# The attention branch product as seven half-size products, its weights prepared earlier, the pooling branch gated on its way out of PSUM

## The chip, the cores and the metric

The kernel runs on one core of one Trainium2 chip. The metric is the time of one execution on the device in microseconds; the kernel before takes 1549.38 us, the median of 3 runs (1548.54 to 1550.18). PE is TensorE (PEld its weight loads), DVE is VectorE, ACT is ScalarE, POOL is GpSimd, and SP is SyncE, which here only issues DMAs.

## The reference, cut to what matters

One residual layer on x of 1024 tokens by 1024 channels, in float32. A pooling branch and a differential attention branch are each projected to 1024 channels, multiplied by their sigmoid gates, and added; then come an output projection and an MLP.

```
gates = jax.nn.sigmoid(h @ w_gate[l] + b_gate[l])
merged = (gates[..., :D_MODEL] * (y_pool @ w_branch_pool[l])
          + gates[..., D_MODEL:] * (y_attn @ w_branch_attn[l]))
x = x + merged @ w_out[l]

h2 = rmsnorm(x, g_ffn[l])
x = x + jnp.square(jax.nn.relu(h2 @ w_up[l])) @ w_down[l]
```

`y_attn` is 1024 tokens by 1024 (8 heads of 128), `w_branch_attn` is 1024 by 1024, `y_pool` is 1024 by 512.

## The kernel before

All products work on digits: `split` makes of a float32 tile a high part (a cast to fp32r on ACT) and a low part (a subtraction on DVE, or on POOL for most weights), and `mm3` adds three matmuls, high x high, high x low, low x high (L126 to L128), into one bank of PSUM. There are eight banks of 128x512.

The stages in order of time:

- **Heads** (until about 626 us). For each of 8 heads and 8 blocks of 128 tokens: the q/k/v projection (tile z), its preparation (a root mean square with POOL's `ms`, the scaling `qn` on DVE and POOL), transposes of q and k (tile tk), scores, exponentials, transposes of the scores, the product with v. The stages of several token blocks are in flight at once; the list `ORDER` sets their lags. Each head's output y goes to DRAM (`y_dram`), its row factors to `r_dram`.
- **Gate columns and pooling groups**, written behind the heads in the program and taken up by PE between their work, and alone until 701 us. A gate column is two fills of 24 matmuls; its bias is added on ACT (`go`, L757) and the result, not yet through the sigmoid, is stored in `g_dram`. The pooling branch's results go to `p_dram`.
- **Pooling products** (tile bp, 701 to 745 us): 8 blocks of 128 output channels by two halves of 512 tokens, 4 depth steps each. ACT copies each bank to `mp`. Meanwhile the heads' y are loaded, multiplied by their row factors (`y_scaled`) and split (`yT`), and the weights of the attention branch are loaded and split (`load_cols`).
- **Attention products** (tile ba, 745 to 832 us): again 8 blocks by two halves, with 8 depth steps. DVE multiplies the bank by its gate (`mg`, L844), POOL adds the gated pooling part (L845), and ACT and DVE split the sum into `mT`. The pooling part is gated in place on DVE (`mp`, L837).
- **Output projection** (tile op, from 832 us), first for tokens 0 to 511, then the rest; behind it the norm and the MLP, whose two large products already are made of seven half-size products each (`SIDES`, `u_product`, `d_product`).

The framework orders each engine's instructions by a planner: a ready instruction that was written earlier in the program goes first. On the chip each engine, and each DMA queue, then works strictly in the planned order. Nearly all loads are issued from SP's queue, so a load that waits for its buffer holds back the loads behind it.

Buffers that matter here: `W` (8 tiles, the head weights, later y and the branch weights), `fw` (4 tiles, the gate weights, later branch and output weights), `fr` and `fo` (2 tiles each, used in turn by `tmp`), `U` (11 tiles of the heads), `H` (`hp0` and `hp1`, first h, then the pooling operand, `mp` and `mT`).

Of the kernel before, what the change touches and what calls it, by code (L numbers as in the profile page):

```python
# [8 lines left out]
F32 = mybir.dt.float32  # L9
# [8 lines left out]
P = 128  # L18
# [19 lines left out]
N_QKVW = 8 * H  # L38
ROOMS = "WWFFWWWFFWWW"
N_AHEAD_Y = 4  # L40

# [16 lines left out]
def encoder_kernel(  # L58
# [31 lines left out]
    hp0 = [mix.enter_context(tc.tile_pool(name=f"hp0{i}", bufs=4)) for i in "ab"]  # L90
    hp1 = mix.enter_context(tc.tile_pool(name="hp1", bufs=8))
    wpool = mix.enter_context(tc.tile_pool(name="wpool", bufs=1))
# [7 lines left out]

    hcount = [0]

    def htile(shape, dt, name, th):

        if th == 0:
            hcount[0] += 1
        return (hp1 if th else hp0[(hcount[0] - 1) // 4 % 2]).tile(shape, dt, tag="H", name=name)

# [3 lines left out]
    def raw(shape, name):  # L112
        return rpool.tile(shape, F32, tag="raw", name=name)
# [4 lines left out]
    def split(hi, lo, src, lo_eng=None):  # L118

        nc.scalar.copy(hi, src)  # L120
        (lo_eng or nc.vector).tensor_tensor(lo, src, f(hi), op=ALU.subtract)  # L121
# [7 lines left out]

    wcount = [0]  # L130

    def wt(shape, name):

        wcount[0] += 1
        if wcount[0] > N_QKVW and ROOMS[(wcount[0] - N_QKVW - 1) // 2] == "F":
            return fw_tile(shape, name)
# [13 lines left out]

    def load_cols(src, c0, name, nk=NK):

        rw = raw([P, nk, P], f"r{name}")
        nc.sync.dma_start(rw, src[0 : nk * P, c0 : c0 + P].rearrange("(kk p) c -> p kk c", p=P))
        ws = []
        for j in range(0, nk, 4):
            w = wt([P, 2, 4, P], f"w{name}_{j}")
            split(w[:, 0], w[:, 1], rw[:, j : j + 4, :], nc.gpsimd)
            ws.append(w)
        return ws  # L160

    def load_cols2(src, c0, name):

        rw = raw([P, 4, 2 * P], f"r{name}")
        nc.sync.dma_start(rw, src[0 : 4 * P, c0 : c0 + 2 * P].rearrange("(kk p) c -> p kk c", p=P))
        ws = []
        for j in range(2):
            w = wt([P, 2, 4, P], f"w{name}_{j}")
# [48 lines left out]

    def gate(gts, c):
        for gt, c0, c1 in gts:
            nc.sync.dma_start(gt, g_dram[c * P : (c + 1) * P, c0:c1])  # L220
            nc.scalar.activation(gt, gt, AF.Sigmoid, bias=zero)

    def whole(g):
        return [(g, 0, S)], [g[:, 0:512], g[:, 512:S]]

    def pair(t):
        return t[:, 0, :], t[:, 1, :]

    def branch_pool(d, ws, ps_fn):

        m = htile([P, S], F32, f"mp{d}", 1)
        for th in range(2):
            ps = proj_T(ps_fn(f"bp{d}_{th}"), ws, lambda k, th: pair(ypT[k][th]), th, nk=4)
            nc.scalar.copy(m[:, th * 512 : (th + 1) * 512], ps)
        mp.append(m)
# [516 lines left out]
    def gate_cols(c):  # L752
        ws = fill_w(w_gate, c * P, f"gate{c}")
        for th in range(2):
            ps = fill_proj(ws, th, f"g{c}_{th}", spare_bank if c >= G_Z else fill_bank)
            fo = fo_tile(f"go{c}_{th}")
            nc.scalar.activation(fo[:, 0:512], ps, AF.Identity, bias=cols[:, c : c + 1])  # L757
            nc.scalar.dma_start(g_dram[c * P : (c + 1) * P, th * 512 : (th + 1) * 512], fo[:, 0:512])
            yield

    def gates():
        for c in range(2 * NK - 2):
            yield from gate_cols(c)
        for gen in [gate_cols(c) for c in (2 * NK - 2, 2 * NK - 1)] * 2:
            next(gen)
            yield

    gate_units = gates()
    for _ in range(G_FIRST):
        next(gate_units)  # L770
    for g in range(4):
        for _ in pool_group(g):
            next(gate_units)
    for _ in gate_units:
        pass


    vpool = attn.enter_context(tc.tile_pool(name="vpool", bufs=N_V))
    pb = mix.enter_context(tc.tile_pool(name="pb", bufs=5, space=PSUM))
    nbank = [0]  # L780

    def vt(shape, dt, name):
        return vpool.tile(shape, dt, tag="V", name=name)

# [9 lines left out]

    def yt_tile(d):
        fn = ut if d < N_YU else vt
        return lambda shape, dt, name, th: fn(shape, dt, name)
# [5 lines left out]
    nbank.append(0)  # L803


    def row_factors(d):
        if d < N_AHEAD_Y or d == 5:
            return [fu_tile(f"rb{d}")]
        if d == 4:
            return [ut([P, S], F32, f"rb{d}")]  # L810
        return [tmp(f"rb{d}_{i}") for i in range(2)]

    ws_bp = {0: load_cols2(w_branch_pool, 0, "bp0")}
    ys = {d: y_scaled(d, row_factors(d)) for d in range(N_AHEAD_Y)}
    ypT = [load_split(p_dram, g * P, f"ypT{g}", ypt_tile) for g in range(4)]
    mp, yT, ws_ba = [], [], {}

    for d in range(NK):
        if d % 2 == 0 and d + 2 < NK:
            ws_bp[d + 2] = load_cols2(w_branch_pool, (d + 2) * P, f"bp{d + 2}")  # L820
        elif d > NK - 4:
            j = len(ws_ba)
            ws_ba[j] = load_cols(w_branch_attn, j * P, f"ba{j}")
        branch_pool(d, ws_bp[d - d % 2][d % 2], bank)
        yT.append(split_halves(ys.pop(d), f"yT{d}", yt_tile(d)))
        if d + N_AHEAD_Y < NK:
            ys[d + N_AHEAD_Y] = y_scaled(d + N_AHEAD_Y, row_factors(d + N_AHEAD_Y))
    mT = {}
    for d in range(NK):
        if d + 3 < NK:  # L830
            ws_ba[d + 3] = load_cols(w_branch_attn, (d + 3) * P, f"ba{d + 3}")
        ws = ws_ba.pop(d)
        gp = [tmp(f"gp{d}_{th}") for th in range(2)]
        gate([(gp[0], 0, 512), (gp[1], 512, S)], d)
        for th in range(2):
            mh = mp[d][:, th * 512 : (th + 1) * 512]
            nc.vector.tensor_tensor(mh, mh, gp[th], op=ALU.mult)  # L837
        ga = fu_tile(f"ga{d}") if d % 2 else ut([P, S], F32, f"ga{d}")
        gate(whole(ga)[0], NK + d)
        for th in range(2):  # L840
            hs = slice(th * 512, (th + 1) * 512)
            ps = proj_T(bank(f"ba{d}_{th}"), ws, lambda k, th: pair(yT[k][th]), th)
            mg = tmp(f"mg{d}_{th}")
            nc.vector.tensor_tensor(mg, ps, ga[:, hs], op=ALU.mult)  # L844
            nc.gpsimd.tensor_tensor(mg, mg, mp[d][:, hs], op=ALU.add)  # L845
            t = htile([P, 2, 512], F32R, f"mT{d}_{th}", th)
            split(t[:, 0, :], t[:, 1, :], mg)
            mT[d, th] = t

    attn.close()
# [481 lines left out]
```

## Time and profile before

| | |
|---|---|
| median of 3 runs | 1549.38 us |
| the profiled execution | 1548.34 us, of which the span is 1546.6 us |
| PE busy / DVE / ACT / POOL | 1526.0 / 1012.4 / 816.5 / 350.9 us |
| pooling products | 701.5 to 745.2 us |
| attention products | 745.2 to 832.2 us |
| bytes moved | 206.41 MB, 133 GB/s over the span |

The profile comes from one execution. Its page gives each engine's busy time, the span in 40 slices, the chain of work that ended last, and groups of instructions by line, engine and tile. A row of a group reads: line, engine, operation, output<-inputs, shape, count | busy us, mean ns of one | idle time of the engine just before them, and who ended it. Other views give the busy time of each engine in chosen stretches, the instructions of one tile with their first and last start, the waits between engines, and the instructions of one engine in order of time. Matmuls overlap, and their ends are modelled, so the distance between starts tells more than a duration.

### The profile page before, as it was taken

The page shows a single profiled execution, that of the slowest core. Times are in us where ns is not written, and L with a number is a line of the kernel's source. Part 1 is how long each engine was busy: PE and PEld are TensorE (multiplying, and loading weights), DVE is VectorE, ACT ScalarE, POOL GpSimd, SP SyncE. Part 2 cuts the span into 40 slices and gives each one's busy share as a digit, 9 for nine tenths or more (in the row PEclk, how much of TensorE's full clock was granted, in tenths as well). Part 3 has the DMA queues.
Part 4 walks back from the last instruction along what each step waited for, and adds up shares of the span by engine and source line. Part 5 has one row for each costly group of instructions (what it writes and reads, how often), then busy time and mean ns, then how long its engine had stood idle before and what let it go on. Part 6 is the DMA issues. An engine that isn't in the chain of part 4 may idle for free.

```text
span 1546.6 us, 22053 instructions
## 1 busy us (share of the span) xinstructions
PE 1526.0 (99%) x7649; PEld 1320.4 (85%) x7649; DVE 1012.4 (65%) x2268; ACT 816.5 (53%) x1808; POOL 350.9 (23%) x448
## 2 busy tenths in 40 slices
PE   7999999999999999999999999999999999999999
PEld 6899999999998989888888887888888788888887
DVE  7777777777878787865322448766666668556672
ACT  6656555666666565566432546565555634333331
POOL 6433334243525262315443400000000000000000
PEclk9999999999999999999999999999999999999999
DMA  7111212020202031547426534555432789537650
GB/s 230 49 54 48 64 39 73 20 79 32 81 28 84 28 96 42 177 132 250 139 93 205 177 105 124 180 172 176 137 136 109 259 312 389 196 123 256 225 192 28
DMA packets 166681, 206.41 MB, mean 133 GB/s; under 512 B 10069, under 2 KB 102954, under 8 KB 166570
## 3 DMA queue, kind: packets, MB, share of 16 engines
q1 hardware_dynamic: 149162, 177.71, 34.8%
q10 hardware_dynamic: 17408, 27.30, 4.7%
q8 instruction: 60, 0.98, 0.3%
q14 instruction: 51, 0.42, 0.1%
HBM read 150.42 MB, written 54.56 MB: 133 GB/s over the span
## 4 chain that ended last, share of the span: by engine, by line
PE 91%; DVE 3%; issue 2%; ACT 1%; DMA 1%; POOL 1%; SPq 1%; POOLq 0%; DVEq 0%; ACTq 0%
PE z L126 5%; PE z L128 5%; PE z L127 5%; PE Da L126 4%; PE Da L127 4%; PE Da L128 4%; PE g L126 3%; PE g L127 3%; PE g L128 3%; PE Db L126 3%; PE Db L127 3%; PE Db L128 3%; PE X L126 2%; PE X L128 2%; PE X L127 2%; PE sc L512 2%
## 5 line engine op out<-in xcount | busy, mean ns | idle before, releaser
L126 PE MATMUL z<-wqkv,hT 128*128 128x384 f32 x512 | 174.5, 341 | 0.4 <-DVE qn L453 0.3
L128 PE MATMUL z<-wqkv,hT 128*128 128x384 f32 x512 | 174.1, 340 | 0.0
L127 PE MATMUL z<-wqkv,hT 128*128 128x384 f32 x512 | 173.8, 339 | 0.0
L522 ACT ACTIVATE s<-s,nm 128x256 f32<-128x256 f32 (+7 forms) x128 | 99.6, 778 | 45.8 <-DVE nm L514 42.7
L260 POOL TENSOR_TENSOR ms<-ms,mhalf 128x4 f32<-128x4 f32 x64 | 66.5, 1039 | 158.0 <-DVE ms L259 136.7
L126 PE MATMUL g<-hT,fwgate 128*128 128x512 f32 x256 | 101.0, 395 | 0.1
L127 PE MATMUL g<-hT,fwgate 128*128 128x512 f32 x256 | 101.0, 395 | 0.0
L128 PE MATMUL g<-hT,fwgate 128*128 128x512 f32 x256 | 101.0, 395 | 0.0
L126 PEld LDWEIGHTS z<-wqkv,hT 128*128 128x128 f32 x512 | 96.8, 189 | 3.9 <-DVE qn L453 1.0
L127 PEld LDWEIGHTS z<-wqkv,hT 128*128 128x128 f32 x512 | 96.6, 189 | 3.0
L128 PEld LDWEIGHTS z<-wqkv,hT 128*128 128x128 f32 x512 | 96.6, 189 | 2.2 <-DVE hT L121 0.5
L514 DVE CUSTOM_DVE_ANT_0 s<-sc,dist 128x512 f32<-128x512 f32 (+3 forms) x128 | 74.7, 586 | 19.7 <-PE sc L512 18.2
L121 POOL TENSOR_TENSOR wqkv<-rqkv,wqkv 128x384 fp32r<-128x384 f32 x60 | 64.0, 1085 | 19.2 <-ACT wqkv L120 15.5
L121 DVE TENSOR_TENSOR AS<-s,AS 128x512 fp32r<-128x512 f32 x64 | 43.9, 688 | 35.8 <-ACT AS L120 35.6
L511 PE MATMUL sc<-K,Q 128*128 128x512 f32 (+2 forms) x192 | 66.6, 353 | 0.1
L512 PE MATMUL sc<-K,Q 128*128 128x512 f32 (+2 forms) x192 | 66.5, 354 | 0.0
L459 POOL TENSOR_TENSOR qn<-qn,ggh 128x128 f32<-128x128 f32 x64 | 32.3, 505 | 138.7 <-DVE qn L453 127.7
L485 ACT CAST Q<-tk 64x128 fp32r<-64x128 f32 x128 | 33.2, 259 | 57.8 <-DVE Q L484 56.0
L482 ACT CAST Q<-tk 64x128 fp32r<-64x128 f32 x128 | 33.0, 258 | 53.7 <-DVE K L481 52.3
L121 POOL TENSOR_TENSOR fwgate<-frgate,fwgate 128x512 fp32r<-128x512 f32 x32 | 44.5, 1394 | 51.9 <-ACT fwgate L120 51.8
L128 PEld LDWEIGHTS g<-hT,fwgate 128*128 128x128 f32 x256 | 48.1, 188 | 8.6
L126 PEld LDWEIGHTS g<-hT,fwgate 128*128 128x128 f32 x256 | 48.2, 188 | 7.3 <-ACT go L757 0.4
(430 smaller groups left out, 4640.7 us busy)
## 6 DMA issues: line engine op xcount, KB each, us to landing
wd<-in_w_down_dram SPq DMA_DIRECT2D x56, 512.0 KB, 5.3
wu<-in_w_up_dram SPq DMA_DIRECT2D x32, 512.0 KB, 4.5
udS<-us SPq DMA_DIRECT2D x64, 256.0 KB, 2.4
ur<-udS SPq DMA_DIRECT2D x32, 512.0 KB, 3.3
rqkv<-in_w_in_dram SPq DMA_DIRECT2D x64, 192.0 KB, 2.7
ud<-u ACTq DMA_DIRECT2D x48, 256.0 KB, 2.1
ur<-ud SPq DMA_DIRECT2D x24, 512.0 KB, 4.7
frgate<-in_w_gate_dram SPq DMA_DIRECT2D x32, 256.0 KB, 2.6
```

Of the source, the lines that this page charges most:

```text
L121: (lo_eng or nc.vector).tensor_tensor(lo, src, f(hi), op=ALU.subtract)
L126: nc.tensor.matmul(ps, lhs_hi, rhs_hi, start=first, stop=False, **kw)
L127: nc.tensor.matmul(ps, lhs_hi, rhs_lo, start=False, stop=False, **kw)
L128: nc.tensor.matmul(ps, lhs_lo, rhs_hi, start=False, stop=last, **kw)
L260: nc.gpsimd.tensor_tensor(dst, dst, mhalf[:, :n], op=ALU.pow)
L459: nc.gpsimd.tensor_tensor(qn[:, 2:4, :], qn[:, 2:4, :], ggh.unsqueeze(1).broadcast_to([P, 2, HD]), op=ALU.mult)
L482: nc.scalar.copy(q_hi, q)
L485: nc.scalar.copy(Q[other, m, 1, :], q)
L511: nc.tensor.matmul(dst, Q[:, i, 0, :], rhs, start=True, stop=False)
L512: nc.tensor.matmul(dst, Q[:, i, 1, :], rhs, start=False, stop=True)
L514: nc.vector.tensor_tensor_reduce(out=s[i][:, c : c + w], in0=sc[:, 0:w], in1=dist[:, o0 + c : o0 + c + w], scale=2.0 ** -(h + 1), scalar=B ...
L522: nc.scalar.activation(s[i][:, 0:n], s[i][:, 0:n], AF.Exp, bias=last, scale=-1.0, accum_out=Z[:, i, t : t + 1])
```

## The change

The product of the 1024 by 1024 weights with the 1024 by 1024 y is taken apart into two by two halves and made of seven half-size products instead of eight, by sums of weight halves (side a) and of y halves (side b). A half-size product has 4 depth steps by 4 column blocks by 3 matmuls of 128x512. They run in the order 1, 2, 6, 7, 5, 4, 3 (`ORDER_BA`), in turn on two sets of four banks (`Xb`, `Yb`); 6, 5, 4 and 3 are added into what their banks hold.

- Side a: eight `weight_unit`s, hung on gate steps 3, 5, 6, 8, 9, 11, 12, 13, load pieces of `w_branch_attn`, make the sums on POOL and the digits on ACT and POOL, and store them in `wa_dram`. `load_a` loads one depth step's digits (512 KB) three steps ahead.
- Side b: all eight y are loaded and scaled and kept in `W`; `split_b` splits a half for one step, five steps ahead, and makes the sums in place on DVE.
- `after` takes each product out of PSUM: copies on ACT, additions, gating and splitting as before.
- The pooling branch is gated as it leaves PSUM (`gate_half`, DVE) instead of copied by ACT and gated later; gate halves come through `tmp`.

The diff, cut to its core:

```diff
-ROOMS = "WWFFWWWFFWWW"
-N_AHEAD_Y = 4
+N_AHEAD_B, N_AHEAD_A = 5, 3
+PREP_AT = (3, 5, 6, 8, 9, 11, 12, 13)
...
     def branch_pool(d, ws, ps_fn):
         m = htile([P, S], F32, f"mp{d}", 1)
+        gs_ = [gate_half(d, th) for th in range(2)]
         for th in range(2):
             ps = proj_T(ps_fn(f"bp{d}_{th}"), ws, lambda k, th: pair(ypT[k][th]), th, nk=4)
-            nc.scalar.copy(m[:, th * 512 : (th + 1) * 512], ps)
+            nc.vector.tensor_tensor(m[:, th * 512 : (th + 1) * 512], ps, gs_[th], op=ALU.mult)
         mp.append(m)
...
+    def weight_unit(src, digits, kk, ch):
+        cs = slice(ch * 256, (ch + 1) * 256)
+        q = fq.tile([P, 4, 256], F32, tag="mx", name=f"wq{kk}_{ch}")
+        for i in range(2):
+            r0 = (kk + 4 * i) * P
+            nc.sync.dma_start(
+                q[:, i::2, :], src[r0 : r0 + P, :].rearrange("p (i c) -> p i c", i=2)[:, :, cs]
+            )
+        a11, a12, a21, a22 = (q[:, i, :] for i in range(4))
+        buf = fu_tile(f"wd{kk}_{ch}").rearrange("p (s h c) -> p s h c", s=2, h=2)
+        def put(j, a):
+            d = buf[:, nput[0] % 2]
+            nput[0] += 1
+            split(d[:, 0, :].bitcast(F32R), d[:, 1, :].bitcast(F32R), a, nc.gpsimd)
+            nc.sync.dma_start(digits[ORDER_BA.index((j, kk))][:, :, cs], d)
+        def minus(o, x_, y_):
+            nc.gpsimd.tensor_tensor(o, x_, y_, op=ALU.subtract)
+        put("1", a11)
+        minus(a21, a11, a21)
+        put("7", a21)
...
+        nc.gpsimd.tensor_tensor(a11, a11, a21, op=ALU.add)
+        put("5", a11)
...
+        if steps[0] in PREP_AT:
+            with tc.issue_after(stored["go"]):
+                weight_unit(w_branch_attn, wa_dram, *units_left.pop(0))
...
+    def gate_half(r0, th):
+        gt = tmp(f"g{r0}_{th}")
+        nc.sync.dma_start(gt, g_dram[r0 * P : (r0 + 1) * P, th * 512 : (th + 1) * 512])
+        nc.scalar.activation(gt, gt, AF.Sigmoid, bias=zero)
+        return gt
...
+    def first_sums(kk):
...
+        nc.vector.tensor_tensor(b12, b22, b12, op=ALU.subtract)
+        nc.vector.tensor_tensor(t2, b12, b11, op=ALU.add)
+    def second_sums(kk):
...
+        nc.vector.tensor_tensor(b11, b22, sums[kk], op=ALU.subtract)
+        nc.vector.tensor_tensor(b21, b21, sums[kk], op=ALU.subtract)
...
+    def load_a(n):
+        wa_ba[n] = wa = (ut([P, 2, 512], F32R, f"wa{n}") if n < 8 or n > 23 else fw_tile([P, 2, 512], f"wa{n}"))
+        nc.sync.dma_start(f(wa), wa_dram[n])
+    def split_b(n):
...
+        yb_ba[n] = yb = vpool.tile([P, 2, 512], F32R, tag="B", name=f"yb{n}", bufs=6)
+        split(yb[:, 0, :], yb[:, 1, :], b)
+        if j == "2":
+            first_sums(kk)
+            second_sums(kk)
+    def ba_step(banks, n):
...
+        for dd in range(4):
+            c = slice(dd * P, (dd + 1) * P)
+            mm3(
+                banks[dd], wa[:, 0, c], wa[:, 1, c], yb[:, 0, :], yb[:, 1, :],
+                not acc and kk == 0, kk == 3, acc,
+            )
+    def gated(d, th, c, src=None):
+        nc.vector.tensor_tensor(c, src or c, gate_half(NK + d, th), op=ALU.mult)
+        nc.gpsimd.tensor_tensor(c, c, mp[d][:, th * 512 : (th + 1) * 512], op=ALU.add)
...
     for d in range(NK):
...
-        yT.append(split_halves(ys.pop(d), f"yT{d}", yt_tile(d)))
+        if d == 1:
+            for k in (6, 7):
+                yr[k] = y_scaled(k, row_factors(k))
+        load_a(d)
+        if d > 2:
+            split_b(d - 3)
+    Yb = [bank(f"baY{dd}") for dd in range(4)]
+    Xb = [bank(f"baX{dd}") for dd in range(4)]
...
+    def after(j):
+        if j == "1":
+            copies("x1", Xb, [h_slab(f"x1_{i}") for i in range(2)])
+        elif j == "2":
+            for dd, c in plus("x1", Yb):
+                gated(dd, 0, c)
+                merged(dd, 0, c)
...
+        elif j == "4":
+            for dd, c in plus("U2", Yb):
+                gated(4 + dd, 0, c)
+                merged(4 + dd, 1, kept_ba["z7"][dd])
+                merged(4 + dd, 0, c)
+        else:
...
+                gated(dd, 1, c, Xb[dd])
+                merged(dd, 1, c)
+    for n, (j, kk) in enumerate(ORDER_BA):
+        if 8 <= n + N_AHEAD_A < 28:
+            load_a(n + N_AHEAD_A)
+        if n + N_AHEAD_B < 28:
+            split_b(n + N_AHEAD_B)
+        ba_step(Xb if j in "1653" else Yb, n)
+        if kk == 3:
+            after(j)
```

More of the change, by code (lines that the diff above doesn't have):

```diff
@@ L774, in encoder_kernel @@
[L774 to L778 removed]
+            gate_step()
+    while gate_step():
+        pass
+    assert not units_left
+    vpool = attn.enter_context(tc.tile_pool(name="vpool", bufs=1))
     pb = mix.enter_context(tc.tile_pool(name="pb", bufs=5, space=PSUM))
[L780 to L783 removed]
+    nbank = [0, 0]
     def bank(name):
```

139 lines of the change are left out of this document (71 added, 68 removed).

## The prediction

> **What bounds the kernel now.** I read, in this order, the page's shares, slices and chain, then the waits of PE, then the busy time by stage, then the rows of the products themselves.
>
> ```profile
> PE 1526.0 (99%) x7649; PEld 1320.4 (85%) x7649; DVE 1012.4 (65%) x2268; ACT 816.5 (53%) x1808; POOL 350.9 (23%) x448
> ...
> POOL 6433334243525262315443400000000000000000
> PEclk9999999999999999999999999999999999999999
> ...
> PE 91%; DVE 3%; issue 2%; ACT 1%; DMA 1%; POOL 1%; SPq 1%; POOLq 0%; DVEq 0%; ACTq 0%
> ```
>
> PE is busy for 99% of the span, the clock is full in every slice, and 91% of the chain that ended last is matmuls. A busy PE is not yet a PE at its peak, so the waits come next:
>
> ```profile
> PE hps L286 <- DVE hn L281: 9.6, 2, 8.9
> PE X L126 <- ACT U L1094: 1.6, 1, 1.6
> ```
>
> Nearly all that PE waits for is the first norm of x at the start (9.6 us); the next largest wait, in the MLP, is 1.6 us. By stage (columns: bounds in us, length, then busy us and instructions of PE, PEld, DVE, ACT, POOL, the clock, DMA share, GB/s), for a stretch of the heads, the pooling products, the attention products, and the down projection:
>
> ```profile
> 280.00:340.00 60.00, 60.00 (x347) 55.43 (x346) 44.50 (x153) 37.31 (x110) 26.21 (x36) 1.00 0.20 61
> ...
> 701.50:745.20 43.70, 43.70 (x194) 36.06 (x194) 21.42 (x30) 28.52 (x48) 18.59 (x14) 1.00 0.64 209
> 745.20:832.20 87.00, 87.00 (x385) 72.07 (x384) 24.30 (x34) 30.89 (x47) 44.11 (x34) 1.00 0.34 110
> ...
> 1242.00:1546.00 304.00, 300.75 (x1327) 248.69 (x1325) 181.82 (x172) 104.61 (x104) 0.00 (x0) 1.00 0.61 215
> ```
>
> In all four PE is busy without a gap (the last row has 1327 matmul records of the 1344 that the program issues there). In the attention products (the stage that is rewritten) DVE, ACT and POOL are busy for 28%, 36% and 51%: there is room beside PE.
>
> **The product that goes.** Tile ba is the attention branch product, op the output projection behind it (durations min/median/max in ns, first and last start):
>
> ```profile
> L126 PE MATMUL ba<-yT,wba x128: 389/389/389, 745.2 to 831.6; 128*128 128x512 f32 x128
> ...
> L128 PE MATMUL ba<-yT,wba x128: 389/389/389, 745.7 to 832.0; 128*128 128x512 f32 x128
> ...
> L126 PE MATMUL op<-wo,mT x128: 389/389/481, 832.3 to 924.2; 128*128 128x512 f32 x128
> ```
>
> The 128 starts of L126 are (831.6 - 745.2) / 127 = 0.680 us apart, with three matmuls in each: 0.2268 us per matmul (the 389 ns is latency, not pitch). Before there are 3 x 128 = 384. After there are 7 products x 4 depth steps x 4 column blocks x 3 = 336, of the same shape. So 48 go, 48 x 0.2268 = 10.9 us; the stage becomes 336 x 0.2268 = 76.2 us, a product 10.9 us, a depth step of 12 matmuls 2.72 us. No matmul is added elsewhere, and the pooling products keep theirs. The same seven-product form runs in the down projection: 7 x 8 x 8 x 3 = 1344 matmuls there, which by this pitch need 304.8 us, and the stage spans about 304. So the form by itself holds the pitch.
>
> That is the whole gain; everything else can only cost. Its lower bound is therefore -10.9 us, apart from the small stalls of before.
>
> **Heads: weight sums and digits move here.** Eight units, each with 2 loads, 7 splits (an ACT copy and a POOL subtraction of 128x256), 4 more POOL operations of 128x256, and 7 stores on SP. No row has that POOL shape; the nearest are:
>
> ```profile
> L121 POOL TENSOR_TENSOR wqkv<-rqkv,wqkv 128x384 fp32r<-128x384 f32 x24 | 24.5, 1043 | 1.4 <-ACT wqkv L120 1.4
> L459 POOL TENSOR_TENSOR qn<-qn,ggh 128x128 f32<-128x128 f32 x24 | 11.6, 484 | 51.7 <-DVE qn L453 46.9 <-PE g L128 4.7
> ...
> L120 ACT CAST oqs<-oq 128x256 fp32r<-128x256 f32 x12 | 4.9, 410 | 0.1
> ```
>
> Between 484 and 1043 ns I take the middle, 0.76 us: 11 x 0.76 = 8.4 us of POOL per unit (5.3 to 11.5), 67 us in all; ACT 7 x 0.41 = 2.9 us per unit, 23 us. The units hang on gate steps 3 to 13. The bias operations (go) of the gate steps start at
>
> ```profile
> L757 ACT ACTIVATE go<-g,cols x4: 687/694/700, 42.8 to 96.7; 128x512 f32<-128x512 f32 x4
> ...
> L757 ACT ACTIVATE go<-g,cols x5: 684/689/702, 223.1 to 316.5; 128x512 f32<-128x512 f32 x5
> ```
>
> so the units spread from about 80 to 310 us. POOL goes from 44% busy (26.21 of 60) to 44 + 67/230 = 73%, ACT from 62% to 72%. What they can delay is the q/k preparation, whose last POOL step (qn) feeds a transpose on PE (tk). One of the tightest pairs I found:
>
> ```profile
> 220.26 0.47 POOL L459 TENSOR_TENSOR qn<-qn,ggh 128x128 f32<-128x128 f32 x1 [6.43 <-DVE qn L453]
> ...
> 224.55 0.38 PE L471 MATMUL tk<-identf,qn 128*128 128x128 f32 x2
> ```
>
> qn ends at 220.73, tk starts at 224.55: 3.8 us to spare. One unit operation ahead of each of the two POOL steps of that chain (ms, qn) delays it by at most 2 x 0.76 = 1.5 us. So I cost the heads at 0 to 2 us and take 0.5. If the cover is gone, that is rival 1. SP also waits here, for each store's subtraction; behind it stand the loads of head weights and gate weights, which are buffered a head or a gate column ahead.
>
> **Pooling products.** Evacuation moves from ACT (copy) to DVE (multiply out of PSUM), with a gate half loaded and passed through the sigmoid for each; the splits of attn weights leave; y 6 and 7 are scaled after block 1.
>
> ```profile
> L844 DVE TENSOR_TENSOR mg<-ba,ga 128x512 f32<-128x512 f32 x16 | 11.0, 689 | 14.5 <-PE ba L128 14.5
> ...
> L221 ACT ACTIVATE gp<-gp,zero 128x512 f32<-128x512 f32 x16 | 11.5, 723 | 11.3 <-DMA gp<-g_dram 11.2
> ...
> 715.28 0.86 SPq L214 DMA_DIRECT2D rb<-r_dram  x2
> ...
> gp<-g_dram SPq DMA_DIRECT2D x16, 256.0 KB, 3.6
> ```
>
> DVE: 16 x 0.69 = 11 us, five operand splits and four sums 9 x 0.69 = 6.2, y 6 and 7 about 4: 21 of 43.7 us, as before. The gate halves turn in four buffers: 3.6 landing + 0.72 + 0.69, some 5 to 6 us a turn, one half per 1.4 us where 2.72 is wanted. They fall behind once, when y 7's factors (loaded at 715 before) borrow the same buffers; eight PSUM banks hold 21.8 us of products, so PE does not see it. What is late next is the start of attention: its first step writes four banks, the fourth of which held the last pooling half. That half ends with the stage; the fourth bank is wanted 9 x 0.2268 = 2.0 us later; the multiply takes 0.69 behind at most one other operation. 0 to 2 us, I take 0.5.
>
> **Attention stage.** Per operation:
>
> ```profile
> L121 DVE TENSOR_TENSOR yT<-ry,yT 128x512 fp32r<-128x512 f32 x16 | 14.6, 937 | 2.1 <-ACT yT L120 2.1
> L121 DVE TENSOR_TENSOR mT<-mg,mT 128x512 fp32r<-128x512 f32 x15 | 10.4, 693 | 40.5 <-ACT mT L120 40.5
> L845 POOL TENSOR_TENSOR mg<-mg,mp 128x512 f32<-128x512 f32 x16 | 20.6, 1285 | 22.5 <-DVE mg L844 19.4 <-DMA ro<-in_w_out_dram 3.0
> L121 POOL TENSOR_TENSOR wo<-ro,wo 128x512 fp32r<-128x512 f32 x12 | 15.4, 1283 | 15.1 <-ACT wo L120 14.9
> L120 ACT CAST mT<-mg 128x512 fp32r<-128x512 f32 x15 | 9.3, 622 | 38.9 <-POOL mg L845 38.9
> L234 ACT COPY mp<-bp 128x512 f32<-128x512 f32 x16 | 8.9, 575 | 1.9 <-PE bp L128 1.9
> ...
> rba<-in_w_branch_attn_dram SPq DMA_DIRECT2D x8, 512.0 KB, 4.7
> ```
>
> DVE: 28 splits, 16 sums, 12 additions out of PSUM, 16 gate multiplies, 16 output splits = 88; 9 lie ahead of the stage and 8 behind it, 71 within: 71 x 0.69 = 49 of 76.2 us; with the 59 that read SBUF twice at the yT price, 12 x 0.69 + 59 x 0.937 = 63.6. ACT: 23 casts and 12 merged splits x 0.62, 12 copies x 0.575, 16 sigmoids x 0.72 = 40 us. POOL: 12 additions x 1.285 = 15.4 plus w_out splits. All fit, on average. Three places are tighter.
> (a) Weight loads: 4 buffers, three steps ahead, 3 x 2.72 = 8.2 us against 4.7 landing: 3.5 us to spare for SP's order. 0 to 6 us, I take 0.5.
> (b) Each product's bank is evacuated under the next one: 10.9 us for 4 operations. Nothing.
> (c) The end. The output projection needs mT[4..7] of the first half, made from the sixth product while the seventh (10.9 us) runs. DVE: 4 x (0.69 + 3 x 0.69) = 11.0 us, and behind the last multiply 1.285 + 0.62 + 0.69. It is wanted 2.7 us (mT[4]) to 4.8 us (mT[7]) after the seventh ends, since four blocks of the first half are already there. About even: 0 to 4 us, I take 0.5.
>
> The Trainium skill, page "SBUF — State Buffer", section "Who interferes with whom", says that a VectorE operation with two SBUF inputs and a GpSimd operation that reads SBUF exclude each other for a whole instruction. The rows agree in part: yT averages 937 ns while POOL works beside it, mT 693 where POOL is waiting for it. By the rule in full the sum would be that of rival 2, 1546 us; by the mT price it stays at 1540.5.
>
> **Sum.** 1546.6 - 10.9 + 0.5 + 0.5 + 0.5 + 0.5 = 1537.7 us of span. The profiled execution took 1548.34 us, 1.74 outside its span, and the median shown, 1549.38, lies 1.04 above it: 1537.7 + 1.74 + 1.04 = 1540.5 us, 0.6% faster.
>
> **Rivals.**
> 1. Slower: the units block POOL in the heads. If a unit's 8.4 us stand as one block ahead of ms or qn, the transpose is late by 8.4 - 3.8 = 4.6 us; eight times 37 us, 1576 us. Half of that per unit gives 18 us, 1558. It decides from 10.9 / 8 = 1.4 us per unit upwards. For it: POOL is strictly in order and waits on ACT copies and on stores. Against: POOL idles 56% there and the operations are short. 11%.
> 2. DVE becomes the bound in attention. If every POOL operation (12 additions, 12 w_out splits) holds DVE for its 1.28 us: 49 + 30.8 = 79.8 us, 3.6 above PE's 76.2, and the end (c) late by 3 more: 1540.5 + 6 = 1546. Against: PE-side gaps only arise where backlog lasts longer than the five steps of prepared operands (13.6 us). 10%.
> 3. Late buffers: SP's order makes gate or weight loads miss by 0.3 us in 15 to 20 steps, 5 us: 1545. For it: the digits add 56 stores of 256 KB and 28 loads of 512 KB, 29 MB, and SP's queue waits for DVE more often. 13%.
> 4. No gain: the stage was not paced by PE after all, 1549. The Trainium skill, page "Perfetto Trace Analysis", section "Identifying the Most-Contended Engine", distrusts matmul busy time and goes by the share of peak and by weight-load busy time. By that the stage is at 72.07 / 87.00 = 83%. Against: durations without spread, no PE wait in it, a constant pitch. 4%.
>
> **Chances.** The forecast's own case (1537.5 to 1543.5) has 62%. 0.2% (3.1 us) is about what can be told from no change here. Faster: 62 + 11 of rival 3 + 8 of rival 2 + 1 of rival 1 = 82%. Same: 9%, from rivals 2, 3, 1 and all of 4. Slower: 9%, rival 1. Range 1537 to 1548 leaves out rival 1, rival 4's upper half and little else.
>
> **What would show it.** Right: 336 matmuls in ba with starts 0.680 us apart per three, op starting some 10 us earlier, heads ending within 2 us of before. Wrong: PE waits at tk on POOL qn between 80 and 310 us (rival 1); PE waits on yb splits or on DVE at the first op rows (rival 2); on wa loads, or on DVE gating at the first attention step (rival 3).

## The result and the profile after

The changed kernel takes 1560.29 us (median of 6 runs, 1558.39 to 1561.88) against 1549.2 us beside it: ratio 1.0071, 95% interval 1.0058 to 1.0084. It is slower by 0.7%; 1540.5 us, faster by 0.6%, had been forecast. The profiled execution took 1558.39 us with a span of 1556.6 us, 10.0 above that of before. The first and last starts of the tiles cut the two profiled spans into stages:

| stage, us | before | after | difference |
|---|---|---|---|
| heads, until the gate columns end | 701.3 | 713.4 | +12.1 |
| pooling products (with the step between) | 43.9 | 45.9 | +2.0 |
| attention products | 87.1 | 76.7 | -10.4 |
| output projection | 92.4 | 95.4 | +3.0 |
| norm and MLP to the end | 621.9 | 625.2 | +3.3 |

The forecast saving is there but for 0.5 us. Every other stage lost. The page of the changed kernel, first the shares and slices, then the chain that ended last:

```profile
PE 1521.2 (98%) x7601; PEld 1310.7 (84%) x7601; DVE 1055.0 (68%) x2309; ACT 832.5 (53%) x1864; POOL 400.2 (26%) x520
...
PE   7999999999999999999999998999999999999999
...
POOL 6446767451526252312037400000000000000000
...
PE 47%; DMA 2%; DVE 2%; issue 2%; ACT 1%; POOL 1%; SPq 0%; POOLq 0%; ACTq 0%; DVEq 0%
```

PE is busy for less time than before (1521.2 us against 1526.0) in a longer span: its idle time grew by 14.8 us. That is not the whole loss, since the matmuls that went should have taken 10.9 us of busy time with them and only 4.8 are gone; the other 6 us lie in rows that count as busy though the matmuls in them start further apart. The slices are too coarse to place the loss, and the chain breaks off (its shares add up to some 55%), so it doesn't lead back into the heads. The busy time by stretch does (columns as in the prediction), for the heads, pooling, attention, and the output projection:

```profile
100.00:340.00 240.00, 232.20 (x1339) 211.77 (x1338) 168.80 (x548) 152.78 (x451) 144.12 (x195) 1.00 0.37 120
280.00:340.00 60.00, 57.09 (x330) 51.98 (x329) 43.37 (x144) 37.70 (x114) 33.88 (x45) 1.00 0.29 91
...
713.50:759.30 45.80, 44.30 (x197) 36.00 (x195) 25.87 (x41) 15.43 (x25) 7.84 (x7) 1.00 0.62 219
759.30:835.80 76.50, 76.50 (x336) 62.75 (x336) 51.22 (x59) 40.03 (x70) 30.87 (x21) 1.00 0.62 210
835.80:931.00 95.20, 93.07 (x432) 76.22 (x431) 51.10 (x73) 43.71 (x84) 32.96 (x28) 1.00 0.56 183
```

The same stretch of the heads before:

```profile
100.00:340.00 240.00, 239.41 (x1393) 221.34 (x1393) 174.00 (x576) 142.93 (x416) 87.28 (x120) 1.00 0.17 53
```

Between 100 and 340 us, where the weight units run, PE lost 7.2 us of busy time (232.20 for 239.41) and 54 matmuls. POOL rose from 87 to 144 us of 240 and ACT from 143 to 153: neither is near full. In the attention stage PE is busy for all of its 76.50 us, with the 336 matmuls that were expected. The waits of PE and, between 80 and 345 us, those of ACT and POOL (us in all, times, longest):

```profile
PE X L125 <- ACT U L1202: 2.9, 1, 2.9
PE ta L543 <- DVE s L507: 2.7, 1, 2.7
...
PE op L127 <- DVE mT L120: 1.7, 2, 0.9
...
PE bp L125 <- DVE mp L210: 1.5, 1, 1.5
...
PE tk L447 <- ACT Q L461: 1.2, 1, 1.2
```

```profile
ACT wd L119 <- DMA wa_dram<-wd: 28.1, 25, 3.1
```

```profile
POOL wd L120 <- ACT wd L119: 30.8, 20, 3.4
```

PE's own list shows many short waits on many tiles and no tk waiting on POOL's qn. ACT's list shows a new one at its top: 25 times it stood at a unit's cast (`wd`, L119 is the cast in `split`), until a store had emptied the digit buffer: 28.1 us. Not all of that is a loss: ACT waits less than before for DVE's parts of Q and K (26.2 us, before 47.4), and PE lost some 7 us in this stretch. How such a wait reaches PE shows best at the transposes `tk`, in order of time:

```profile
273.66 0.40 ACT L119 CAST wd<-wq 128x256 fp32r<-128x256 f32 x1 [1.07 <-DMA wa_dram<-wd]
273.97 0.26 ACT L461 CAST Q<-tk 64x128 fp32r<-64x128 f32 x1
274.28 0.44 PE L447 MATMUL tk<-identf,qn 128*128 128x128 f32 x2 [1.17 <-ACT Q L461]
```

The unit's cast waits 1.07 us for a store; the cast of Q stands behind it in ACT's order; and PE stands for 1.17 us until that cast is done. The longest wait in the heads (`ta`, 2.7 us at 204.55) has a longer path: ACT stood 2.00 us at a unit's cast until 192.88, worked without a gap from 194.28 on, and so was late with the cast of K at 196.88, for which DVE waited 1.10 us; DVE was then late for the exponential at 200.77, which waited 1.32 us for it, and behind that come DVE's work on `s` and the transposes. Of the eight stalls of PE over 0.35 us between 100 and 345 us, 7.6 us in all, four (5.2 us) lead back in this way to a unit's cast that had waited for a store. In what follows W is this explanation (a unit's cast waits on ACT for a store), O that the units' mere occupancy of the engines costs the time, P that POOL's share of the units blocks the heads (the prediction's rival 1).

### The profile page after: what moved, and what is told of

It is laid out like the page before. It is cut to its first block, busy times and chain, and to the rows that moved or that the text cites. A ratio compares the mean times of both kernels' runs of the same rounds, so it can differ in the third digit from the quotient of the medians.

```text
span 1556.6 us, 22409 instructions
## 1 busy us (share of the span) xinstructions
PE 1521.2 (98%) x7601; PEld 1310.7 (84%) x7601; DVE 1055.0 (68%) x2309; ACT 832.5 (53%) x1864; POOL 400.2 (26%) x520
## 4 chain that ended last, share of the span: by engine, by line
PE 47%; DMA 2%; DVE 2%; issue 2%; ACT 1%; POOL 1%; SPq 0%; POOLq 0%; ACTq 0%; DVEq 0%
PE Da L125 4%; PE Da L127 4%; PE Da L126 4%; PE Db L125 3%; PE Db L127 3%; PE Db L126 3%; PE X L125 2%; PE X L127 2%; PE X L126 2%; PE Z L127 2%; PE Z L126 2%; PE Z L125 2%; PE op L127 2%; PE op L125 1%; PE op L126 1%
## 5 line engine op out<-in xcount | busy, mean ns | idle before, releaser
L457 DVE TENSOR_TENSOR K<-tk,K 64x128 fp32r<-64x128 f32 x128 | 37.0, 289 | 34.2 <-ACT K L456 31.0
L435 POOL TENSOR_TENSOR qn<-qn,ggh 128x128 f32<-128x128 f32 x64 | 32.2, 503 | 101.5 <-DVE qn L429 93.8
```

The lines of the kernel that those rows point to most:

```text
L457: nc.vector.tensor_tensor(K[other, m, c0 : c0 + P], k, f(k_hi), op=ALU.subtract)
```

## Experiments

Diffs are against the changed kernel unless another is named; ratios are to the kernel before, run beside each. A table of all follows at the end.

**The units alone**, in the kernel before: `weight_unit` and its place on the gate steps are added, and nothing reads `wa_dram`.

```diff
+    wa_dram = dram.tile([28, P, 2, 512], F32, name="wa_dram")
+    def weight_unit(src, digits, kk, ch):
...
+        if steps[0] in PREP_AT:
+            with tc.issue_after(stored["go"]):
+                weight_unit(w_branch_attn, wa_dram, *units_left.pop(0))
```

> The kernel before, with the eight weight units of the change added at the same gate steps; nothing reads what they store. Theory W (the units put ACT's copies behind waits for the digit buffers' stores, and the heads end about 12 us later) and theory O (the units' bare work of ACT and POOL does it): 1549 + 12 = 1561 us, 1558 to 1563, the last gate column ends near 713 us instead of 701. Theory B (the loss before the pooling products comes from the new branch stages, which the planner mixes into the heads' end): 1549 to 1551 us, the gate columns end at 701 to 702.

1564.89 us, ratio 1.0101 (1.0086 to 1.0116), above the 1558 to 1563 expected. The units cost 15.7 us without any part of the new products: more than the whole saving. In the profiled execution the heads end 10.6 us later than before (711.9), and the pooling products, which were not expected to change, take 6.4 us longer; their part was not traced further. ACT's wait and PE's busy time are those of the changed kernel:

```profile
ACT wd L121 <- DMA wa_dram<-wd: 28.3, 26, 3.7
```

```profile
100.00:340.00 240.00, 233.12 (x1348) 213.22 (x1347) 170.93 (x550) 153.18 (x451) 145.63 (x195) 1.00 0.38 121
```

So is the order in which PE works through the heads: the two traces agree in 99% of their steps, while that of the kernel before agrees with the changed kernel's in about half. The units bring this order with them, whatever the stages behind the heads are.

**No units**: only two short ones remain, of one split each, so that `wa_dram` is written; all steps load its slab 0. Weight sums and digits are left out.

```diff
         put("1", a11)
+        return
...
-        if steps[0] in PREP_AT:
+        if steps[0] in PREP_AT[:2]:
...
-        nc.sync.dma_start(f(wa), wa_dram[n])
+        nc.sync.dma_start(f(wa), wa_dram[0])
```

> The changed kernel with all weight sums and digits left out but one quarter of one slab (two short units of one split each), so that every step reads the same 512 KB slab; products, loads and the side of y are unchanged. W and O: the gate columns end at 701 to 703 us, total 1560.3 - 12 = 1548 us (1546 to 1550). B: the end stays near 713 us, total 1557 us or more.

1550.79 us, 1.0008 (0.9994 to 1.0022): 9.5 us come back, but the saving still does not show, and both numbers lie above those expected. The heads end at 707.8 us, 6.5 after those of before, without units: between 500 and 701 us PE loses 3.6 us of busy time against before. So the new stages cost the heads something by themselves (B), too.

**Units without their stores**: all ACT and POOL work stays, 2 of 56 stores remain.

```diff
-            nc.sync.dma_start(digits[ORDER_BA.index((j, kk))][:, :, cs], d)
+            if j == "1" and kk == 0:
+                nc.sync.dma_start(digits[0][:, :, cs], d)
...
-        nc.sync.dma_start(f(wa), wa_dram[n])
+        nc.sync.dma_start(f(wa), wa_dram[0])
```

> The changed kernel with all loads, sums, copies and subtractions of the eight units, but only two of their 56 stores; every step reads the same slab. W: the waits of ACT for the stores are gone, so the gate columns end at 702 to 705 us and the total is 1549 to 1552 us. O: the work is the same, so the end stays at 710 to 714 us and the total at 1557 to 1561 us.

1553.09 us, 1.0028 (1.0018 to 1.0037). Without stores 7.2 of those 9.5 us come back although every cast and subtraction is still there; occupancy (O) is left with about the 2.3 us between this kernel and the one without units. The heads end at 709.0 us, between what W (702 to 705) and O (710 to 714) expected; but in the stretch of the units PE is back at its busy time of before (239.41). ACT and PE:

```profile
ACT wd L119 <- DMA wa_dram<-wd: 2.1, 2, 1.5
```

```profile
100.00:340.00 240.00, 239.12 (x1386) 220.15 (x1386) 178.60 (x569) 156.73 (x461) 144.03 (x196) 1.00 0.22 68
```

**A third digit buffer**, with everything stored (the operand buffers of the attention stage go from six to five to make room):

```diff
+        third = fq.tile([P, 2, 256], F32, tag="wd3", name=f"wd3{kk}_{ch}")
...
-            d = buf[:, nput[0] % 2]
+            d = third if nput[0] % 3 == 2 else buf[:, nput[0] % 3]
...
-N_AHEAD_B, N_AHEAD_A = 5, 3
+N_AHEAD_B, N_AHEAD_A = 4, 3
```

> The changed kernel with three instead of two digit buffers for a unit (room for it is made by splitting y four steps ahead instead of five). A buffer returns after three puts of 1.15 us instead of two, against about 3 us of store: the wait per put falls from about 1.9 us at worst to about 0.7. W: a half to two thirds of the 12 us come back, 1552 to 1555 us. O: 1559 to 1561 us.

1548.59 us, 0.9998 (0.9989 to 1.0007): 11.7 us back, more than the half to two thirds of 12 expected, with the same work and the same bytes of stores. In the profiled spans 6.8 us are the heads (706.6 for 713.4) and 3.0 the MLP. ACT's wait (28.1 in the change) and PE:

```profile
ACT wd L119 <- DMA wa_dram<-wd: 9.2, 14, 1.8
```

```profile
100.00:340.00 240.00, 237.26 (x1374) 217.92 (x1373) 174.55 (x569) 158.06 (x464) 143.74 (x197) 1.00 0.37 120
```

One reservation holds for this and the two experiments beside it (no stores, casts on POOL): each also changes the order in which the heads' instructions are planned, and PE's order agrees with the changed kernel's in about half of its steps at most. What the shorter wait gives and what the other order gives is not told apart by them.

**The casts on POOL**, two buffers as in the change, so that POOL and not ACT waits for the stores:

```diff
-            split(d[:, 0, :].bitcast(F32R), d[:, 1, :].bitcast(F32R), a, nc.gpsimd)
+            nc.gpsimd.tensor_copy(d[:, 0, :].bitcast(F32R), a)
+            nc.gpsimd.tensor_tensor(d[:, 1, :].bitcast(F32R), a, d[:, 0, :], op=ALU.subtract)
```

> The changed kernel with two digit buffers as there, but the cast of the high digits in the units made by POOL instead of ACT. Theory W (it is ACT's queue that must not stand behind the stores, since exp and the q/k copies are in it): ACT has no wait left on the stores, POOL takes them, with some 4 us to spare before its transposes; 56 more POOL operations of 0.5 to 0.75 us. 1549 to 1555 us. Rival P (POOL is the engine that hurts, as rival 1 of the prediction had it): POOL is now busy for over 80% there and waits for the stores itself, 1563 us or more.

1555.76 us, 1.0038 (1.0025 to 1.0052), just above W's 1549 to 1555 and far below P's 1563. POOL now stands at the units (`wd` L763) for 32 us, and PE is busier in that stretch than in the kernel before:

```profile
POOL wd L763 <- DMA wq<-in_w_branch_attn_dram: 20.2, 5, 5.6
POOL wd L763 <- DMA wa_dram<-wd: 11.9, 10, 2.3
```

```profile
100.00:340.00 240.00, 239.98 (x1400) 221.55 (x1399) 182.52 (x591) 146.50 (x424) 154.19 (x230) 1.00 0.35 114
```

So P is false for that stretch: a POOL that stands for up to 5.6 us at a time doesn't reach PE there; an ACT that stands for 1.1 us on average does. The heads still end at 710.2 us, by stalls of 0.8 to 2.6 us between 356 and 706 us.

**Repairs behind the heads.** With three buffers the heads are no longer the largest loss, and the next kernels, all with three buffers, work on the others. *The first half first*: `z7` moves to another pool, and the splits of the output projection's first half are written ahead of those of the second.

```diff
-            copies("z7", Yb, [h_slab(f"z7_{i}") for i in range(2)])
+            copies("z7", Yb, [up_slab(f"z7_{i}") for i in range(2)])
...
-                merged(4 + dd, 1, kept_ba["z7"][dd])
                 merged(4 + dd, 0, c)
+            for dd in range(4):
+                merged(4 + dd, 1, kept_ba["z7"][dd])
```

> The three-buffer kernel (1548.6 us), and the seventh product's cover used otherwise: the kept product for the second half goes to another buffer pool, so that the four splits that the output projection waits for come ahead of the four that it needs 40 us later. Theory S (DVE and POOL slow each other in that stretch, mT splits take 1.2 to 1.8 us instead of 0.69, and the last one is late): 4 x 1.6 us of DVE leave the path, the two waits of 0.85 and 1.69 us at the first output products go, 1545.5 to 1547 us. Rival: the output projection waits for w_out's digits in truth, 1548.6 as before.

1555.73 us, 1.0037 (1.0025 to 1.0049): 7 us worse than three buffers alone, where 2 to 3 better was expected. The profiled execution was the fastest of its five (1551.57 us, against 1549.60 for three buffers alone), so its trace shows only part of this. The planner still put `z7` splits between those of the first half. PE's waits between 745 and 960 us:

```profile
PE hb L1053 <- DVE y L1050: 2.6, 1, 2.6
...
PE baY L125 <- DMA wa<-wa_dram: 2.0, 1, 2.0
PE op L127 <- DVE mT L120: 1.7, 1, 1.7
```

*Row factors through `fu`*, so that the first gate halves of the pooling stage find a free buffer (three digit buffers as before):

```diff
-        return [fu_tile(f"rb{d}")] if d in (0, 1, 2, 3, 5) else [tmp(f"rb{d}_{i}") for i in range(2)]
+        return [fu_tile(f"rb{d}")] if d < 6 else [tmp(f"rb{d}_{i}") for i in range(2)]
```

> The three-buffer kernel, and one row factor taken through another buffer, so that the first two gate halves load into fr, free some 25 us earlier, and not into fo, which the last gate columns still hold. Theory G (the first pooling bank is emptied 7 us late because its gate waits for the last gate store): the wait of 1.2 us at the pooling products goes, 1547 to 1548 us; ACT's wait for the first gate (6.8 us in the changed kernel) goes with it. Rival: the wait is for another bank, no change.

1548.27 us, 0.9994 (0.9985 to 1.0004), like three buffers alone and a little above the 1547 to 1548 expected. A stall of 1.11 us at the pooling products stays, against 1.66 in the change; that late gate halves are its whole cause is not shown. *Both edits together:*

> Three buffers, early gates and the first half first together. S and G: 1548.6 - 2.5 - 1.2 = 1545 us, 1544 to 1546.5, faster than the kernel before (1549.2). If neither holds: 1548.6.

1549.86 us, 1.0004 (0.9995 to 1.0013), not the 1544 to 1546.5 expected of both. The pooling stall is gone, but PE still waits 2.2 us for `mT` and 1.1 us for weights from `wa_dram`. *On top of both, the four additions behind the sixth product move from POOL to DVE*, and the second half's splits, with the last product's gating, are held until the first half's splits are issued:

```diff
-                gated(4 + dd, 0, c)
-                merged(4 + dd, 0, c)
+                gated(4 + dd, 0, c, eng=nc.vector)
+                kept_ba["end"] = merged(4 + dd, 0, c)
+            with tc.issue_after(kept_ba["end"]):
+                for dd in range(4):
+                    merged(4 + dd, 1, kept_ba["z7"][dd])
```

> On the kernel of e8 (three digit buffers, early gates): in the seventh product's cover the four gate additions go from POOL to DVE, and the splits for the second half of the tokens are held back until the four wanted ones are issued. Theory C (DVE operations with two SBUF inputs and POOL operations exclude each other there, 1.77 and 1.75 us each instead of 0.69 and 1.29): POOL has only the w_out splits left there, the splits mT of the first half come below 1.3 us, the output products' waits on mT (2.2 us) go, and the norm's wait behind them too: 1545 to 1547.5 us against 1549.9 for e8. Rival: DVE is bound by its own count of operations, the waits on mT stay at 2 us or grow, 1549 to 1551.

1546.59 us (1544.25 to 1552.3), 0.9989 (0.9979 to 0.9999), within what was expected: the best version found, by its median 0.1% below the kernel before. The interval only just leaves out no difference, and this is the best of several versions picked afterwards, so that it is faster than before is not shown. The output projection takes 92.9 us instead of 95.5, and PE no longer waits for `mT`. The profile shows why. DVE and POOL around the end of the attention stage in the changed kernel:

```profile
834.60 1.78 DVE L120 TENSOR_TENSOR mT<-z,mT 128x512 fp32r<-128x512 f32 x1
836.31 1.77 DVE L120 TENSOR_TENSOR mT<-bU,mT 128x512 fp32r<-128x512 f32 x1
```

```profile
828.98 1.75 POOL L120 TENSOR_TENSOR wo<-ro,wo 128x512 fp32r<-128x512 f32 x1
830.68 1.75 POOL L897 TENSOR_TENSOR bU<-bU,mp 128x512 f32<-128x512 f32 x1
```

and DVE in the version with the additions on it:

```profile
828.64 0.68 DVE L120 TENSOR_TENSOR mT<-bU,mT 128x512 fp32r<-128x512 f32 x1
...
829.84 1.28 DVE L120 TENSOR_TENSOR mT<-bU,mT 128x512 fp32r<-128x512 f32 x2
```

Side by side, each engine's operation lasts 1.75 to 1.78 us; with POOL out of the way DVE's lasts 0.68. (An x2 row spans two instructions.) POOL stood idle from 826.4 to 830.9 us there. With work taken from POOL and given to the busier engine, operations of both became shorter. What the holding back of the second half's splits adds was not run by itself.

**Deeper weight loads**, on both edits: five steps ahead, with digits in more buffers.

```diff
-N_AHEAD_B, N_AHEAD_A = 4, 3
+N_AHEAD_B, N_AHEAD_A = 4, 5
...
-        wa_ba[n] = wa = (ut([P, 2, 512], F32R, f"wa{n}") if n < 8 or n > 23 else fw_tile([P, 2, 512], f"wa{n}"))
+        wa_ba[n] = wa = (ut([P, 2, 512], F32R, f"wa{n}") if n < 8 or n > 23 or n % 2 else fw_tile([P, 2, 512], f"wa{n}"))
```

> On the kernel of e8: weight digits of every second step go to another buffer pool, and loads run five steps ahead instead of three. Theory L (three steps are too few where a load lands after 6.0 us and SP is held up): the wait of 1.1 us on wa goes, 1548.5 us. Rival: SP's queue holds the loads back whatever their buffers, no change.

1551.65 us, 1.0019 (1.0010 to 1.0028), 3 us above the 1548.5 expected. The wait for weights is gone, and the output projection grows to 101.5 us, with a stall of 5.8 us ahead of the norm at 870.7 us. *With the DVE additions as well:*

> Both together on the kernel of e8. C and L: 1544.5 to 1547 us, below the kernel before (1549.0). Where it stays at 1549 or above, the rest of the loss lies in the heads and in the MLP's clock, not in these waits.

1548.65 us, 0.9999 (0.9988 to 1.0010), above the 1544.5 to 1547 expected, PE waiting once at the norm for 4.4 us:

```profile
PE hb L1055 <- DVE y L1052: 4.4, 1, 4.4
```

**What is left in the heads.** Two kernels from the best version: the unit casts on POOL (the edit above), and no units at all (the edit above; weight sums and digits left out).

> The kernel of e9 (three digit buffers, early gates, four additions on DVE), with the units' casts on POOL. If ACT's remaining waits for the stores are what the heads still lose, the stretch from 40 to 340 us has no stall of PE above 0.25 us and the gate columns end near 703 us instead of 706.7: 1543 to 1546 us. If the rest comes from other places of the heads, which another plan of the same work makes by itself, the end stays at 705 to 710 us and the total at 1546 to 1550.

> The kernel of e9 with the weight units left out but two short ones, every step reading the same slab: the branch part alone, with its waits mended. If the units still cost 4 to 5 us there, 1541 to 1543 us, near the forecast of the prediction. If the planner's other order of the heads costs as much without them, 1545 to 1548 us with the gate columns ending at 705 us or later.

Casts on POOL: 1552.11 us, 1.0021 (1.0012 to 1.0030), heads ending at 709.1 us. No units: 1552.57 us, 1.0025 (1.0016 to 1.0034), heads ending at 707.0 us. Both are slower by 5.5 to 6 us than the version with all units, and above every range that was expected. The heads do not show why: against 706.7 us their ends are 2.4 and 0.3 us later, less than the scatter named below the table, and the profiled executions (1547.47 and 1549.98 us) lie close to that of the best version (1548.92). Some of it is the clock: its mean over the runs is 0.9971 and 0.9966, in the best version 0.9977, worth 0.9 to 1.7 us; the rest is open. Taking the work away did not give a floor: PE is busier where the units were and loses elsewhere. The stretches of 500 to 640 us and 640 to 701 us without units:

```profile
500.00:640.00 140.00, 137.16 (x779) 124.32 (x778) 110.54 (x338) 84.66 (x244) 56.08 (x76) 1.00 0.29 95
640.00:701.00 61.00, 59.07 (x298) 49.44 (x297) 32.56 (x82) 28.44 (x57) 10.89 (x10) 1.00 0.55 186
```

and in the best version, with units:

```profile
500.00:640.00 140.00, 138.89 (x805) 127.58 (x803) 113.50 (x353) 81.70 (x242) 53.08 (x74) 1.00 0.23 76
640.00:701.00 61.00, 61.00 (x319) 51.70 (x318) 39.54 (x97) 34.23 (x75) 9.24 (x11) 1.00 0.61 200
```

All versions (us; heads end and output projection from the profiled execution):

| kernel | median | heads end | output projection |
|---|---|---|---|
| before / after | 1549.2 / 1560.29 | 701.3 / 713.4 | 92.4 / 95.4 |
| units alone in before | 1564.89 | 711.9 | 92.4 |
| no units / no stores | 1550.79 / 1553.09 | 707.8 / 709.0 | 95.5 / 95.4 |
| three buffers / casts on POOL | 1548.59 / 1555.76 | 706.6 / 710.2 | 97.0 / 99.5 |
| first half first / row factors / both | 1555.73 / 1548.27 / 1549.86 | 702.8 / 703.3 / 706.4 | 99.5 / 97.1 / 95.5 |
| both + DVE additions | 1546.59 | 706.7 | 92.9 |
| deeper loads / with DVE additions | 1551.65 / 1548.65 | 705.1 / 704.0 | 101.5 / 98.6 |
| best + casts on POOL / best, no units | 1552.11 / 1552.57 | 709.1 / 707.0 | 93.1 / 94.1 |

Among the versions with three buffers and the casts on ACT, edits that touch nothing ahead of the pooling stage still move the end of the heads by some 4 us (702.8 to 706.7). Another order of instructions is not the reason: in their traces PE, ACT, DVE and POOL each work through the heads in the same order in all seven, but for the last steps. Each version was profiled once, so this is most likely the scatter of single executions. A difference of that size between two versions is not read as the effect of the edit.

## Why the prediction was wrong, by its own steps

**"The product that goes": right.** 48 matmuls fewer, -10.9 us forecast, -10.4 measured (76.7 us for 336 matmuls, 76.2 forecast), at the same pitch. DVE's 51.22 us in that stage lie near the lower of its two estimates (49 and 63.6).

**"Heads": the step that failed.** 0.5 us was taken, from 0 to 2; 12.1 us were measured. The prices of the operations were good:

```profile
L119 ACT CAST wd<-wq x56: 391/407/428, 81.4 to 300.7; 128x256 fp32r<-128x256 f32 x56
...
L120 POOL TENSOR_TENSOR wd<-wq,wd x56: 723/739/1255, 81.9 to 301.2; 128x256 fp32r<-128x256 f32 x56
```

0.41 and 0.74 us, where 0.41 and 0.76 had been taken. The engines were less full than forecast: between 100 and 340 us POOL was busy for 60% and ACT for 64%, not 73% and 72%. What failed is that occupancy was the only thing asked about ACT: its wait for the digit buffers stood at nothing in the sum. `put` turns two buffers, and each is free again only after a cast (0.41), a subtraction (0.74) and a store:

```profile
wa_dram<-wd SPq DMA_DIRECT2D x56, 256.0 KB, 2.4
```

0.41 + 0.74 + 2.4 = 3.55 us by medians for two casts, 1.8 us a cast, for an engine that could make one each 0.41 us and has the exponentials of the heads behind it. The prediction saw waits for stores on SP and POOL, and checked the slack of one chain, through POOL to `tk` (3.8 us); the wait stands on ACT, whose chains to PE go through the casts of Q and K (to `tk` and, by DVE, to the next `z`) and through `s` to `ta`. All the numbers for that sum but the store's landing time stood in the diff and the rows shown.

How much of the 12.1 us this wait is, the runs tell only in part. The units alone, in the kernel before, put the end of the heads 10.6 us later. The third buffer gave back 6.8 in the heads, the missing stores 4.4, the casts on POOL 3.2, each give or take the scatter of some 4 us and each with another order of instructions. In the stretch of the units all three come close to the kernel before (237.26, 239.12 and 239.98 us of PE for 239.41, the change 232.20). What they leave lies behind that stretch: without units the heads still ended 6.5 and 5.7 us after before. The two parts do not add up to 12.1 (10.6 and 6.5 would be 17.1), and where the second comes from stays open; since the units move the heads with the pools and loads of before as well, the new pools and loads can't be the cause of the first.

**"Pooling products": 0.5 taken, 2.0 measured,** at the upper bound. The loss is at the start of the stage, not at the start of attention, where it was placed (the stage behind shows no idle time). The first gate half came late on ACT, its multiply followed, and PE waited 1.5 us for that multiply (`bp` in the list above). ACT and DVE at that place:

```profile
722.20 0.72 ACT L824 ACTIVATE g<-g,zero 128x512 f32<-128x512 f32 x1 [6.81 <-DMA g<-g_dram]
722.95 0.69 DVE L210 TENSOR_TENSOR mp<-bp,g 128x512 f32<-128x512 f32 x1 [5.75 <-ACT g L824]
```

**"Attention stage" (a), weight loads: right for this kernel, with less to spare than reckoned.** Nothing was waited for, but a load took 6.0 us from issue to landing, not 4.7, of the 8.2 available. In six versions that reach the stage earlier, PE waits 1 to 2.5 us for one of them between 800 and 809 us. **(b): right.** **(c), the end: 0.5 taken, 3.0 measured,** within its 0 to 4; PE's waits for `mT` there are 2.2 us of it. It was found even because additions and splits were priced at 0.69 and 1.285 us; beside each other they took 1.75 to 1.78.

**The MLP was not in the sum.** 3.3 us: two stalls that before had as well grew (by the distances of PE's starts 1.84 us for 0.95 near 967 us, 3.10 for 1.80 near 1243 us), and one stretch of 3.4 us ran at half clock, which costs 1.7 us by itself, as shown below. Why the two stalls grew is not shown. The stage was taken to be free of gaps to begin with: the prediction says that PE is busy without a gap in all four of its stretches, but its last row, in the MLP, has 300.75 us of 304.

**The rivals.** Rival 1 had the right stage, sign and size (1558 to 1576, "1.4 us per unit upwards"; 12.1 / 8 = 1.5), but the wrong engine: POOL, as the kernel with casts on POOL shows, has the room it was credited with. It got 11% since the argument against it, POOL's idle 56%, was an argument about that engine alone. Rival 2's mechanism is real, but PE stood only at the end, and not in the stage. The exclusion rule of the Trainium skill ("SBUF — State Buffer", "Who interferes with whom") was set aside for the `mT` price; the 1.75 to 1.78 us of both engines side by side, against 0.68 alone, agree with it. Rival 3 came true in small, at the first gate half. Rival 4 is out: the stage became shorter by 10.4 of 10.9 us.

## What to carry to other kernels

Work that is put into the gaps of an engine that works in order can cost more than its busy time, namely the time for which it stands at the head of the queue: for each added instruction, reckon when its buffer comes back (with a store, the landing time counts), and then look for who stands behind it. Buffers used in turn, with a DMA in each turn, want more than two, or belong on an engine whose successors have slack; here one more buffer of 256 KB, with the other order of instructions that came with it, gave back 11.7 us of 1560, 6.8 of them in the heads. And an even balance at a stage's end, priced from operations that ran alone, was a loss here, where two engines ran side by side. Where a trace leads back from a stalled matmul to an instruction that waited, that is worth more than the difference of two versions whose instructions are planned in different orders.

## What the hardware showed that was not expected

Short stalls of PE can cost twice. Around 953 us in the changed kernel, PE in order of time, and the clock by stretch:

```profile
953.09 0.50 PE L125 MATMUL Y<-B21h,A 128*128 128x512 f32 x1 [0.83 <-DVE u L971]
...
954.91 0.63 PE L125 MATMUL Y<-B21h,A 128*128 128x512 f32 x1
955.34 0.63 PE L126 MATMUL Y<-B21l,A 128*128 128x512 f32 x1
```

```profile
945.00:952.00 7.00, 5.45 (x27) 3.94 (x25) 7.00 (x13) 2.75 (x6) 0.00 (x0) 1.00 0.36 112
952.00:954.20 2.20, 1.37 (x6) 0.94 (x6) 2.20 (x5) 2.20 (x6) 0.00 (x0) 1.00 0.00 0
954.20:957.60 3.40, 3.40 (x10) 2.63 (x9) 3.05 (x6) 3.40 (x8) 0.00 (x0) 0.50 0.02 5
```

After stalls of 1.7 and 1.1 us, the clock stands at 0.50 for 3.4 us and matmuls start 0.43 us apart instead of 0.227: 1.7 us lost on top. It isn't certain to follow. The same pair of stalls stands at this place in all fifteen profiled executions of this case, and in seven of them, the changed kernel's among them and the one before not, such a stretch came behind it. Of 24 single stalls longer than 2 us (the distance of two starts less the 0.227 us), 10 had one beside them; of 72 between 0.5 and 1 us none had. The Trainium skill ("TensorE: Matmul & The Clock Gate", "Why this matters for your kernels") warns of idle gaps above some 3 us; here shorter ones, also two in a row, were enough. Over all runs the mean granted clock was 0.9992 before (96 runs beside the experiments) and 0.9977 after (6 runs); the difference of 0.0015 is worth some 2.3 us of 1550. Much of the scatter within a version goes with it: the best version with casts on POOL took 1547.47 us at a clock of 0.999 and 1555.31 at 0.994, and 0.005 of 1550 us is 7.8.
